# In the delta net, GpSimd's products go to ScalarE and VectorE, and a transfer that adds makes the low parts of the weights

## The chip, the cores and the metric

The kernel runs on one core of a Trainium2 chip. A time is device microseconds (us) of one launch. Five instruction streams run beside each other on the core: TensorE (PE, with its weight loads shown apart as PEld), VectorE (DVE), ScalarE (ACT), GpSimd (POOL) and SyncE (SP), which here only issues transfers. Each works through its instructions in the order in which the program lists them, and semaphores make one wait for another.

## The reference, cut to what matters

The program is two transformer blocks in float32 on 512 tokens of width 1024. The part that is changed is the second mixer of the first block, a gated delta net with 8 key heads and 16 value heads of width 128:

```python
proj = u @ w_in                                   # 1024 -> 6144 + 32
qkv = silu(causal_dwconv(proj[..., :4096], conv_w))   # four taps over the tokens
q, k = l2_norm(q) * K ** -0.5, l2_norm(k)
beta = sigmoid(b);  g = -exp(a_log) * softplus(a + dt_bias)
decay = exp(where(incl, gc[:, None] - gc[None, :], -inf))   # gc = cumsum(g)
m = where(strict, beta * (k @ k.T) * decay, 0)
u, w = triangular_solve(m + I, [v * beta, k * beta * exp(gc)])
# then the chunks in turn: v_new = u - w S;  o = q_dec S + qk v_new;  S = S g_last + k_dec^T v_new
o = rms_norm(o, norm_gain) * silu(z);   h = h + o @ w_out
```

## The kernel before, in words

Activations lie with features on the 128 partitions and the 512 tokens along the free axis. Every large product is made of three float32r matmuls of 128x512 (`mm3`): each operand is split into a high part, rounded to float32r, and a low part, what is left of it; high by high, high by low and low by high are summed in one PSUM bank. The weights come as 486 blocks of 128x1024 floats (512 KB), each holding eight 128x128 tiles. `wtile` takes a block in: SP loads it into `wr`, ACT rounds it into `wh` (the high part), DVE subtracts, `wl = wr - wh` (the low part). There are three buffers for `wr` and four each for `wh` and `wl` (`WRAW, WPART = 3, 4`), so PE can be up to three blocks behind what ACT and DVE prepare. One block feeds 24 matmuls of 128x512.

Nothing is issued while it is written: a recorder notes each operation with its operands, and a planner (`schedule`) then plays the program with a cost for each operation and fixes the order of every engine's instructions. On the chip that order holds whatever the real durations are. A changed cost or a changed instruction therefore also moves others.

The delta net (`gdn`) takes 65 of the blocks: 49 of `gdn_in` and 16 of `gdn_out`. It works in four rounds of four value heads. A round begins with `keys` for two key heads: each needs two convolutions (`conv`: DVE multiplies the projection by the norm's row R into `g`, ACT starts `y` with the tap of the current token, the three earlier taps are added, ACT takes tanh, DVE finishes the silu), transposes on PE, the decay matrices of two value heads (`G` = triangle times log-decay in a high and a low part, PE sums them in `pd`, ACT takes exp into `E`, `E` is multiplied by beta), and from E the tiles `Y`, `kqd` and `yd`. Then `inverse` solves the unit triangular systems in 31 steps on DVE (`xt`, `xp`), with `xts` and `xf` set to zero by POOL. Meanwhile PE makes the four value projections (`values`) and the output product of the round before (`project`). Last come the four heads (`gdn_head`): a recurrence over four token blocks that goes back and forth between PE, ACT (`gvn`, `ot`) and DVE (`gt`, `St`), with `kd` = keys times decay made beforehand, and the output `ot` scaled by its norm at the end, and the gates (`gates`).

Before, POOL does five kinds of product in this part: the sum of the first tap (`y + w`, with `w` made by ACT), both `G`, `E` times beta, `kd`, and the scaling of `ot`.

Of the kernel before, what the change touches and what calls it, by code (L numbers as in the profile page):

```python
# [8 lines left out]
F32 = mybir.dt.float32  # L9
F32R = mybir.dt.float32r  # L10
BF16 = mybir.dt.bfloat16
I32 = mybir.dt.int32
AF = mybir.ActivationFunctionType
ALU = mybir.AluOpType
# [3 lines left out]
S = 512  # L18
# [142 lines left out]
class Recorder:  # L161
# [104 lines left out]
    def schedule(self):  # L266
# [18 lines left out]
        while done < len(ops):  # L285
# [22 lines left out]
            T, e = best  # L308
# [48 lines left out]
                mode = op.mode  # L357
            if op.eng == "SP" or op.lat < 0:
                start = max(T + 0.1, dma_free)
                dma_free = start + op.cost  # L360
                op.end = dma_free + 2.0
                free[e] = T + 0.06
            else:
                op.end = T + cost + op.lat
                free[e] = T + cost
# [129 lines left out]
class Kernel:  # L495
    def __init__(self, tc, ctx, I, vat, cat):
        self.tc, self.nc, self.I = tc, Recorder(tc.nc), I
        self.vat, self.cat = vat, cat
        self.blocks, self.open, self.wcur = [], None, None
        self.n = 0  # L500
        self.cp = ctx.enter_context(tc.tile_pool(name="cp", bufs=1))
        self.sp = ctx.enter_context(tc.tile_pool(name="sp", bufs=2))
        self.ap = ctx.enter_context(tc.tile_pool(name="ap", bufs=NACT))
        self.pp = ctx.enter_context(tc.tile_pool(name="pp", bufs=8, space=PSUM))
        self.dp = ctx.enter_context(tc.tile_pool(name="dp", bufs=1, space=bass.MemoryType.DRAM))
# [41 lines left out]
    def wtile(self, name, k, m, width=128):  # L547
        nc = self.nc
        if not self.open or len(self.open) == 8:
            self.open = []  # L550
            self.blocks.append(self.open)
            raw = self.wide("wr", F32, ("wr", WRAW))
            hi = self.wide("wh", F32R, ("wh", WPART))
            lo = self.wide("wl", F32R, ("wl", WPART))
            n = len(self.blocks)

            for i, c in enumerate((slice(0, 256), slice(256, 1024)) if n == 1 else (slice(0, 1024),)):
                op = nc.sync.dma_start(out=raw[:, c], in_=self.I["w"][n - 1][:, c])
                if n < 3:
                    op.prio = self.loads[3 * n - 3 + 2 * i].prio + (0.5 if i or n > 1 else -0.5)  # L560
                nc.scalar.copy(hi[:, c], raw[:, c])
                nc.vector.tensor_tensor(lo[:, c], raw[:, c], hi[:, c].bitcast(F32), ALU.subtract)
            self.wcur = (hi, lo)
        j = len(self.open) * 128
        self.open.append((name, k, m))
        return self.wcur[0][:, j:j + width], self.wcur[1][:, j:j + width]
# [397 lines left out]
    def gdn(self):  # L964
# [58 lines left out]

        def conv(m):
            ps = self.gemm("gdn_in", m, xs)
            gt, y, u = self.act(name="g"), self.act(name="y"), self.act(name="w", cap=2)
            nc.vector.tensor_tensor(gt, ps, R, ALU.mult)
            w = lambda t: cw[:, t * 32 + m:t * 32 + m + 1]
            nc.scalar.activation(y, gt, AF.Identity, scale=w(3))
            nc.scalar.activation(u[:, 3:], gt[:, :S - 3], AF.Identity, scale=w(0))  # L1030
            nc.gpsimd.tensor_tensor(y[:, 3:], y[:, 3:], u[:, 3:], ALU.add)
            for t in (1, 2):
                nc.vector.scalar_tensor_tensor(y[:, t:], gt[:, :S - t], w(3 - t), y[:, t:], ALU.mult, ALU.add)
            nc.scalar.activation(gt, y, AF.Tanh)
            nc.vector.scalar_tensor_tensor(y, gt, 1.0, y, ALU.add, ALU.mult)
            return y

        def keys(j, yd):
# [33 lines left out]
            out = []  # L1072
            for i in range(2):
                h = 2 * j + i
                bc = lambda t: t[:, :, h:h + 1].broadcast_to([128, 4, 128])
                pd = self.ps((128, 4, 128))
                Gs = [self.act(F32R, name="G", shape=(4, 128), cap=4) for _ in gparts]
                for G, x in zip(Gs, gparts):
                    nc.gpsimd.tensor_tensor(G, self.c("tri").unsqueeze(1).broadcast_to([128, 4, 128]),
                                            bc(x.bitcast(F32)), ALU.mult)  # L1080
                nc.after = (len(nc.ops) - 1,)
                for part, G in enumerate(Gs):
                    nc.tensor.matmul(pd, ut, G, start=part == 0, stop=part == 1)
                nc.after = ()
                E_ = self.act(name="E", shape=(4, 128), cap=2)
                nc.scalar.activation(E_, pd, AF.Exp)
                nc.gpsimd.tensor_tensor(E_, E_, bc(beta), ALU.mult)
                Y = self.act(name="Y", shape=(4, 128))
                nc.vector.tensor_tensor(Y, E_, kk, ALU.mult)
                kqd = self.act(name="kqd", shape=(4, 128))  # L1090
# [119 lines left out]
    def gdn_head(self, h, kq, kt, vt, kqd, xf, egc, negegc, be, glb, eq):  # L1210
# [1 line left out]
        nc = self.nc  # L1212
        St = self.nc.pool_tile(self.sp, [128, 128], F32, "St", self.nm("St"), 3)
        kd = self.act(name="kd", shape=(4, 128), cap=2)
        nc.gpsimd.tensor_tensor(kd[:, 0:3], kt[:, 0:3], be[:, 0:3, h:h + 1].broadcast_to([128, 3, 128]), ALU.mult)
        ot = self.act(name="ot", shape=(4, 128), cap=3)
        ss = self.small([128, 4], "gss", bufs=3)
        for b in range(4):
# [22 lines left out]
            sq = self.nc.pool_tile(self.sp, [128, 128], F32, "gsq", self.nm("gsq"), 2)  # L1241
            nc.scalar.activation(sq, ot[:, b], AF.Square, accum_out=ss[:, b:b + 1])
        rr = self.rsqrt(ss, [128, 4], 1.0 / 128, eq)
        nc.gpsimd.tensor_tensor(ot, ot, rr.unsqueeze(2).broadcast_to([128, 4, 128]), ALU.mult)
        po = self.ps()
        for b in range(4):
            self.tr(po[:, b * 128:(b + 1) * 128], ot[:, b])
# [336 lines left out]
    def run(self, out, stages):  # L1584
# [12 lines left out]
        for s in stages:  # L1597
            if s != "swa" and ada and not hasattr(self, "cs"):
                self.ada_start()
            if s == "swa":  # L1600
                self.attention()
            elif s in ("ffn0", "ffn1"):
# [86 lines left out]
```

## Time and profile before

| | |
|---|---|
| time, median of 3 runs (lowest to highest) | 2748.89 us (2748.49 to 2749.71) |
| the profiled execution's own time | 2749.72 us |
| its span, first to last instruction | 2747.9 us |
| busy: PE, PEld, DVE, ACT, POOL | 2641.9, 2161.2, 1773.9, 1089.3, 301.7 us |
| mean granted TensorE clock | 0.983 of full |

The delta net lies at about 615 to 1210 us of the span. A granted clock of 1.00 is 2.4 GHz and 0.50 would be 1.2 GHz; a value between is a mean over both levels in that stretch. Matmuls overlap one another, so that the duration of one (385 ns) is longer than the distance between two starts. An idle time is put down to what ended it. A DVE instruction's duration is from its start to its last write, and includes the time for which it is held up by another engine at the memory.

### The profile page before, as it was taken

What the parts mean: (1) busy time and instruction counts of PE and PEld (TensorE: products, weight loads), DVE (VectorE), ACT (ScalarE), POOL (GpSimd) and SP (SyncE); (2) the same over time, 40 slices, a digit from 0 to 9 for tenths busy, and PEclk for the clock granted to TensorE, in tenths of its full rate; (3) what the DMA queues carried; (4) which work ended last, traced back from release to release, by engine and by line L of the source; (5) the groups of instructions that cost most, each with busy time, mean ns of one, the idle gap of its engine ahead of it and who ended that gap; (6) DMA issues with size and microseconds to landing.
All of it is one profiled execution on the core that took longest, in us unless ns stands there. A gap on an engine that the chain in (4) does not pass through costs nothing.

```text
span 2747.9 us, 36693 instructions
## 1 busy us (share of the span) xinstructions
PE 2641.9 (96%) x14108; PEld 2161.2 (79%) x14108; DVE 1773.9 (65%) x3576; ACT 1089.3 (40%) x1969; POOL 301.7 (11%) x333
## 2 busy tenths in 40 slices
PE   7899999997989899999999999999999999999998
PEld 5678878776768677777787898888877778988887
DVE  8977848858798889876546453334479856633334
ACT  5753323334545445543323333223264443432231
POOL 3411101104141414111001000000000000000000
PEclk9999999998899999999999999999999999999999
DMA  4115645641111121123333323233222233233231
GB/s 149 47 62 198 224 138 195 227 134 43 62 46 63 54 67 62 63 87 103 115 102 109 99 92 99 93 100 99 88 89 64 75 108 97 87 98 100 93 100 62
DMA packets 84001, 274.27 MB, mean 100 GB/s; under 512 B 9328, under 2 KB 17776, under 8 KB 83824
## 3 DMA queue, kind: packets, MB, share of 16 engines
q1 hardware_dynamic: 83680, 271.39, 30.5%
q8 instruction: 111, 1.82, 0.3%
q14 instruction: 66, 0.54, 0.1%
q10 hardware_dynamic: 144, 0.52, 0.1%
HBM read 264.54 MB, written 7.34 MB: 99 GB/s over the span
## 4 chain that ended last, share of the span: by engine, by line
PE 73%; DVE 19%; issue 3%; ACT 2%; POOL 1%; DMA 1%; SPq 0%; DVEq 0%; ACTq 0%; POOLq 0%
PE mm L406 66%; PE ps L406 8%; DVE wl L406 3%; DVE y L406 2%; DVE wa L406 1%; DVE yd L406 1%; DVE xl L406 1%; DVE g L406 1%; DVE sm L406 1%; DVE n_4t L406 1%; DVE xt L406 1%; DMA wa<-in_w_dram 1%; DVE Y L406 1%; DVE z L406 1%; POOL n_2t L406 1%
## 5 line engine op out<-in xcount | busy, mean ns | idle before, releaser
L406 PE MATMUL mm<-xh,wh 128*128 128x512 f32 (+1 forms) x3444 | 1322.7, 385 | 16.9 <-ACT xh L406 16.8
L406 PE MATMUL mm<-xl,wh 128*128 128x512 f32 (+1 forms) x3444 | 1326.2, 386 | 1.8 <-DVE xl L406 1.8
L406 PE MATMUL mm<-xh,wl 128*128 128x512 f32 (+1 forms) x3444 | 1323.8, 385 | 2.2 <-DVE wl L406 2.2
L406 PEld LDWEIGHTS mm<-xh,wh 128*128 128x128 f32 x3444 | 651.7, 189 | 142.7 <-ACT xh L406 18.6
L406 PEld LDWEIGHTS mm<-xl,wh 128*128 128x128 f32 x3444 | 652.5, 190 | 132.0 <-issue 7.5
L406 PEld LDWEIGHTS mm<-xh,wl 128*128 128x128 f32 x3444 | 652.3, 190 | 129.0 <-issue 6.3
L406 DVE TENSOR_TENSOR wl<-wr,wh 128x1024 fp32r<-128x1024 f32 (+1 forms) x415 | 521.6, 1257 | 273.9 <-issue 181.3
L406 ACT CAST wh<-wr 128x1024 fp32r<-128x1024 f32 (+1 forms) x415 | 433.6, 1046 | 414.7 <-DVE wl L406 225.3
L406 ACT CAST xh<-g 128x512 fp32r<-128x512 f32 x92 | 57.2, 622 | 250.2 <-DVE g L406 250.0
L406 DVE TENSOR_TENSOR g<-mm,g 128x512 f32<-128x512 f32 x44 | 30.4, 691 | 175.9 <-PE mm L406 175.3
L406 POOL TENSOR_TENSOR y<-y,R 128x512 f32<-128x512 f32 x48 | 67.8, 1413 | 682.8 <-ACT y L406 652.9
L406 DVE CUSTOM_DVE_ANT_0 wa<-wa,cs,vec 128x1024 f32<-128x1024 f32 x72 | 96.9, 1347 | 10.3 <-DMA wa<-in_w_dram 10.1
L406 DVE TENSOR_TENSOR xt<-xt,mm 128x512 f32<-128x512 f32 (+1 forms) x72 | 48.0, 670 | 84.2 <-PE mm L406 83.9
L406 ACT ACTIVATE sq<-xt 128x512 f32<-128x512 f32 (+1 forms) x69 | 38.7, 570 | 148.9 <-DVE xt L406 148.9
L406 DVE SCALAR_TENSOR_TENSOR xt<-mm,mod,xt 128x512 f32<-128x512 f32 (+1 forms) x47 | 31.6, 671 | 101.1 <-PE mm L406 100.8
L406 DVE TENSOR_TENSOR g<-mm,R 128x512 f32<-128x512 f32 x80 | 54.8, 685 | 56.1 <-PE mm L406 53.3
L406 DVE SCALAR_TENSOR_TENSOR y<-g,vec,y 128x511 f32<-128x511 f32 (+1 forms) x96 | 71.7, 749 | 22.8 <-ACT y L406 21.3
L406 DVE TENSOR_TENSOR g<-mm,y 128x512 f32<-128x512 f32 x48 | 33.0, 687 | 61.6 <-POOL y L406 32.2
L406 POOL TENSOR_TENSOR y<-y,w 128x509 f32<-128x509 f32 x32 | 49.5, 1547 | 209.1 <-ACT w L406 123.3
L406 DVE TENSOR_TENSOR xl<-g,xh 128x512 fp32r<-128x512 f32 x92 | 63.0, 685 | 6.9 <-ACT xh L406 6.9
L406 ACT ACTIVATE y<-g,vec 128x512 f32<-128x512 f32 x48 | 39.2, 817 | 67.4 <-DVE g L406 67.4
L406 ACT ACTIVATE g<-mm 128x512 f32<-128x512 f32 x44 | 26.4, 599 | 96.9 <-PE mm L406 96.9
(316 smaller groups left out, 2580.6 us busy)
## 6 DMA issues: line engine op xcount, KB each, us to landing
wr<-in_w_dram SPq DMA_DIRECT2D x413, 512.0 KB, 3.6
wa<-in_w_dram SPq DMA_DIRECT2D x72, 512.0 KB, 4.6
xt<-in_xt_dram SPq DMA_DIRECT2D x8, 256.0 KB, 6.3
bias<-bo SPq DMA_DIRECT2D x8, 256.0 KB, 2.7
bi<-bias SPq DMA_DIRECT2D x8, 256.0 KB, 4.4
out_dram<-fin SPq DMA_DIRECT2D x8, 256.0 KB, 2.6
bias<-bo SPq DMA_DIRECT2D x8, 192.0 KB, 1.9
bi<-bias SPq DMA_DIRECT2D x8, 192.0 KB, 3.9
```

What stands on the lines that cost most here:

```text
L406: fn(*args, **kw)
```

## The change

Six edits in the delta net, and one in the planner.

- The first tap of each convolution: the product `w` on ACT and the sum on POOL go; DVE adds this tap as it adds the other two, with a third SCALAR_TENSOR_TENSOR.
- `G`: one POOL product of 128x512 becomes four ACT products of 128x128, each with a scale per partition. There are 32 `G`.
- `E` times beta: from POOL to DVE, 16 of 128x512.
- `kd`: one POOL product of 128x384 becomes three ACT products of 128x128, for 16 heads.
- `ot` scaled: one POOL product of 128x512 becomes four ACT products of 128x128, for 16 heads.
- The low part of the 65 weight blocks of this part: DVE's subtraction goes. ACT writes `-wh` into `wl`, and POOL issues a transfer that reads the block from DRAM a second time and adds it to what lies in `wl`. 
- The planner: a transfer on POOL holds POOL for 1.1 us, counts twice its bytes and lands 3 us after.

```diff
@@ schedule
-                dma_free = start + op.cost
-                op.end = dma_free + 2.0
-                free[e] = T + 0.06
+                dma_free = start + op.cost * (2 if e == "POOL" else 1)
+                op.end = dma_free + (3.0 if e == "POOL" else 2.0)
+                free[e] = T + (1.1 if e == "POOL" else 0.06)
@@ wtile
                 nc.scalar.copy(hi[:, c], raw[:, c])
-                nc.vector.tensor_tensor(lo[:, c], raw[:, c], hi[:, c].bitcast(F32), ALU.subtract)
+                if self.by_dma:
+                    nc.scalar.activation(lo[:, c], hi[:, c].bitcast(F32), AF.Copy, scale=-1.0)
+                    nc.gpsimd.dma_start(out=lo[:, c], in_=self.I["w"][n - 1][:, c].bitcast(F32R), accum_op=ALU.add)
+                else:
+                    nc.vector.tensor_tensor(lo[:, c], raw[:, c], hi[:, c].bitcast(F32), ALU.subtract)
@@ conv
-            nc.scalar.activation(u[:, 3:], gt[:, :S - 3], AF.Identity, scale=w(0))
-            nc.gpsimd.tensor_tensor(y[:, 3:], y[:, 3:], u[:, 3:], ALU.add)
-            for t in (1, 2):
+            for t in (1, 2, 3):
                 nc.vector.scalar_tensor_tensor(y[:, t:], gt[:, :S - t], w(3 - t), y[:, t:], ALU.mult, ALU.add)
@@ keys
-                    nc.gpsimd.tensor_tensor(G, self.c("tri").unsqueeze(1).broadcast_to([128, 4, 128]),
-                                            bc(x.bitcast(F32)), ALU.mult)
+                    for b in range(4):
+                        nc.scalar.activation(G[:, b], self.c("tri"), AF.Copy, scale=x.bitcast(F32)[:, b, h:h + 1])
-                nc.gpsimd.tensor_tensor(E_, E_, bc(beta), ALU.mult)
+                nc.vector.tensor_tensor(E_, E_, beta[:, :, h:h + 1].broadcast_to([128, 4, 128]), ALU.mult)
@@ gdn_head
-        nc.gpsimd.tensor_tensor(kd[:, 0:3], kt[:, 0:3], be[:, 0:3, h:h + 1].broadcast_to([128, 3, 128]), ALU.mult)
+        for b in range(3):
+            nc.scalar.activation(kd[:, b], kt[:, b], AF.Copy, scale=be[:, b, h:h + 1])
-        nc.gpsimd.tensor_tensor(ot, ot, rr.unsqueeze(2).broadcast_to([128, 4, 128]), ALU.mult)
+        for b in range(4):
+            nc.scalar.activation(ot[:, b], ot[:, b], AF.Copy, scale=rr[:, b:b + 1])
@@ run
+            self.by_dma = s == "gdn"
```

Counted over the whole program, DVE loses 65 subtractions and gains 48 instructions, ACT loses 32 and gains 305, POOL loses 112 products and gains 65 transfers.

Three places in the order show what this does. The first is DVE in the first round, where the decay matrices of the first two heads become `Y`, `kqd` and `yd` (the numbers at the names only tell tiles apart). Before:

```order
L406 TENSOR_TENSOR Y_1145<-E_1144,kk_1137 128x512
L406 TENSOR_TENSOR kqd_1146<-E_1144,qk_1138 128x512
L406 COPY yd_1105<-Y_1145 32x128 x4
L406 TENSOR_TENSOR Y_1151<-E_1150,kk_1137 128x512
L406 TENSOR_TENSOR kqd_1152<-E_1150,qk_1138 128x512
L406 COPY yd_1105<-Y_1151 32x128 x4
L406 TENSOR_TENSOR wl_1266<-wr_1264,wh_1265 128x1024
L406 SCALAR_TENSOR_TENSOR y_1158<-g_1157,gcw,y_1158 128x511
L406 TENSOR_TENSOR g_1164<-mm_1160,R_1082 128x512
L406 SCALAR_TENSOR_TENSOR y_1158<-g_1157,gcw,y_1158 128x510
L406 TENSOR_TENSOR wl_1275<-wr_1273,wh_1274 128x1024
```

And now:

```order
L406 TENSOR_TENSOR E_1142<-E_1142,gbeta_1090 128x512
L406 TENSOR_TENSOR Y_1143<-E_1142,kk_1135 128x512
L406 TENSOR_TENSOR kqd_1144<-E_1142,qk_1136 128x512
L406 COPY yd_1105<-Y_1143 32x128 x4
L406 TENSOR_TENSOR E_1148<-E_1148,gbeta_1090 128x512
L406 SCALAR_TENSOR_TENSOR y_1156<-g_1155,gcw,y_1156 128x511
L406 TENSOR_TENSOR Y_1149<-E_1148,kk_1135 128x512
L406 TENSOR_TENSOR kqd_1150<-E_1148,qk_1136 128x512
L406 COPY yd_1105<-Y_1149 32x128 x4
L406 SCALAR_TENSOR_TENSOR y_1156<-g_1155,gcw,y_1156 128x510
L406 TENSOR_TENSOR g_1161<-mm_1157,R_1082 128x512
L406 SCALAR_TENSOR_TENSOR y_1156<-g_1155,gcw,y_1156 128x509
```

Both `wl` are gone from the list, an `E` stands ahead of each `Y`, and the convolution `y` has a third tap (128x509).

The second place is ACT, a little later in the same round, around the exponentials `E`. Before:

```order
L406 ACTIVATE E_1150<-ps_1147 128x512
L406 CAST wh_1265<-wr_1264 128x1024
L406 ACTIVATE y_1158<-g_1157,gcw 128x512
L406 ACTIVATE w_1159<-g_1157,gcw 128x509
L406 CAST wh_1274<-wr_1273 128x1024
L406 ACTIVATE E_1191<-ps_1188 128x512
```

And now:

```order
L406 ACTIVATE E_1148<-ps_1145 128x512
L406 ACTIVATE G_1185<-cst,ghi_1101 128x128 x3
L406 ACTIVATE G_1186<-cst,glo_1102 128x128 x4
L406 ACTIVATE G_1191<-cst,ghi_1101 128x128 x4
L406 ACTIVATE G_1192<-cst,glo_1102 128x128 x4
L406 ACTIVATE E_1187<-ps_1184 128x512
L406 ACTIVATE wl_1252<-wh_1251 128x1024
L406 ACTIVATE y_1162<-g_1161,gcw 128x512
```

Between two `E` there now stand fifteen small `G` products, and the negated copy `wl` of a block whose `wh` was made thirty rows earlier.

The third place is POOL, at the end of the first round's `keys`. Before:

```order
L406 TENSOR_TENSOR E_1191<-E_1191,gbeta_1090 128x512
L406 TENSOR_TENSOR E_1197<-E_1197,gbeta_1090 128x512
L406 TENSOR_TENSOR kd_1282<-kt_1120,gbe_1098 128x384
L406 TENSOR_TENSOR kd_1317<-kt_1120,gbe_1098 128x384
L406 MEMSET xp_1201 128x512
L406 COPY xp_1201<-cst 128x16 x2
L406 TENSOR_TENSOR y_1259<-y_1259,w_1260 128x509
```

And now:

```order
L406 DMA wl_1303<-in_w_dram 128x1024
L406 DMA wl_1338<-in_w_dram 128x1024
L406 MEMSET xp_1197 128x512
L406 COPY xp_1197<-cst 128x16 x2
L406 DMA wl_1373<-in_w_dram 128x1024
L406 DMA wl_1408<-in_w_dram 128x1024
L406 DMA wl_1417<-in_w_dram 128x1024
L406 DMA wl_1423<-in_w_dram 128x1024
L406 DMA wl_1462<-in_w_dram 128x1024
L406 MEMSET xts_1231 32x16x32
```

POOL's products are gone; its list in this part is the 65 transfers and the inverse's small instructions (`xp`, `xts`, `xf`) among them.

## Rows read from the trace of the kernel before

**Rows 1.** Busy us of PE, PEld, DVE, ACT, POOL; granted clock, DMA share, GB/s

```profile
600.00:1215.00 615.00, 555.85 (x3532) 457.87 (x3532) 520.21 (x1224) 296.69 (x711) 165.43 (x154) 0.94 0.19 61
```

**Rows 2.** The same view, the stretch of `keys` in each of four rounds

```profile
640.00:700.00 60.00, 47.78 (x206) 38.34 (x207) 52.77 (x102) 26.59 (x54) 25.26 (x22) 0.83 0.14 46
780.00:820.00 40.00, 28.02 (x122) 22.00 (x121) 38.58 (x70) 16.25 (x34) 19.62 (x17) 0.85 0.13 40
900.00:960.00 60.00, 49.38 (x233) 39.49 (x233) 53.16 (x100) 28.45 (x59) 26.14 (x25) 0.91 0.16 53
1040.00:1120.00 80.00, 70.18 (x348) 56.58 (x347) 74.48 (x154) 41.01 (x90) 29.88 (x23) 0.98 0.21 66
sum 240.00, PE 195.37 PEld 156.41 DVE 218.99 ACT 112.31 POOL 100.90; mean PE 48.84 PEld 39.10 DVE 54.75 ACT 28.08 POOL 25.23
```

**Rows 3.** Who waited for whom, PE and PEld, 600 to 1215: total us, times, longest

```profile
PE ps L406 <- DVE y L406: 42.0, 15, 6.0
...
PEld ps L406 <- POOL ot L406: 5.4, 6, 3.2
```

**Rows 4.** Timeline, DVE, POOL and PE, 776 to 822: start, us, what [idle before]

```profile
775.22 1.03 DVE L406 SCALAR_TENSOR_TENSOR n_4t<-n_4t,n_4e 128x4 f32<-128x4 f32 x1
...
783.48 2.21 DVE L406 COPY yd<-Y 32x128 f32<-32x128 f32 x3
...
775.18 3.12 POOL L406 TENSOR_TENSOR E<-E,gbeta 128x512 f32<-128x512 f32 x2 [0.91 <-DVE n_4t L406]
...
816.70 1.08 PE L406 MATMUL ps<-cst,y 128*128 128x128 f32 x4 [5.29 <-DVE y L406]
```

**Rows 5.** Groups of instructions, 600 to 1215: count, busy us, mean ns, idle before

```profile
L406 DVE TENSOR_TENSOR wl<-wr,wh 128x1024 fp32r<-128x1024 f32 x70 | 87.3, 1247 | 2.7 <-issue 2.2
L406 ACT CAST wh<-wr 128x1024 fp32r<-128x1024 f32 x69 | 72.1, 1046 | 66.9 <-PE mm L406 57.2 <-DVE xt L406 6.1 <-issue 2.0
L406 DVE SCALAR_TENSOR_TENSOR y<-g,gcw,y 128x511 f32<-128x511 f32 x64 | 58.4, 912 | 7.8 <-POOL y L406 7.5
...
L406 DVE COPY yd<-Y 32x128 f32<-32x128 f32 x64 | 28.4, 444 | 0.7
...
L406 ACT ACTIVATE w<-g,gcw 128x509 f32<-128x509 f32 x32 | 22.7, 710 | 0.0
...
L406 DVE TENSOR_TENSOR n_4t<-n_4y 128x4 f32<-128x4 f32 x78 | 19.4, 255 | 1.1
...
L406 DVE TENSOR_TENSOR Y<-E,kk 128x512 f32<-128x512 f32 x16 | 16.6, 1037 | 1.2 <-POOL E L406 0.9
...
L406 DVE TENSOR_TENSOR kqd<-E,qk 128x512 f32<-128x512 f32 x16 | 15.6, 977 | 0.0
```

**Rows 6.** The tiles `yd`, `y`, `n_4t` and `kqd`, 600 to 1215: duration ns min/median/max

```profile
L406 DVE COPY yd<-Y x64: 206/222/1699, 649.2 to 1096.9; 32x128 f32<-32x128 f32 x64
...
L406 DVE SCALAR_TENSOR_TENSOR y<-g,gcw,y x64: 703/747/1780, 628.5 to 1112.0; 128x511 f32<-128x511 f32 x32, 128x510 f32<-128x510 f32 x32
...
L406 DVE TENSOR_TENSOR n_4t<-n_4y x78: 149/161/1251, 615.6 to 1214.9; 128x4 f32<-128x4 f32 x78
...
L406 DVE TENSOR_TENSOR kqd<-E,qk x16: 677/685/1769, 647.8 to 1095.6; 128x512 f32<-128x512 f32 x16
```

**Rows 7.** The tile `wl` on DVE in the four stretches of rows 2

```profile
sum 240.00, DVE 33.42; mean DVE 8.36
```

**Rows 8.** Timeline of ACT, 640 to 700: four small products with a scale

```profile
684.24 1.14 ACT L406 ACTIVATE vt<-ps,gik 128x128 f32<-128x128 f32 x4 [7.14 <-PE ps L406]
```

**Rows 9.** Transfers: queue totals in 600 to 1215; issues of whole run, KB, us to landing

```profile
q1 hardware_dynamic: 10511, 37.03, 18.9%
...
wr<-in_w_dram SPq DMA_DIRECT2D x413, 512.0 KB, 3.6
...
xt<-in_xt_dram SPq DMA_DIRECT2D x8, 256.0 KB, 6.3
```

**Rows 10.** The chain that ended last, 590 to 1230: matmuls of weight blocks back to back

```profile
834.59 22.96 PE mm L406 x101
```

More of the change, by code (lines that the diff above doesn't have):

```diff
@@ L499, in __init__ @@
         self.blocks, self.open, self.wcur = [], None, None
+        self.by_dma = False
         self.n = 0
@@ L1025, in conv @@
             ps = self.gemm("gdn_in", m, xs)
-            gt, y, u = self.act(name="g"), self.act(name="y"), self.act(name="w", cap=2)
+            gt, y = self.act(name="g"), self.act(name="y")
             nc.vector.tensor_tensor(gt, ps, R, ALU.mult)
@@ L1074, in keys @@
                 h = 2 * j + i
-                bc = lambda t: t[:, :, h:h + 1].broadcast_to([128, 4, 128])
                 pd = self.ps((128, 4, 128))
```

## The prediction

> **What bounds the kernel now.** I read the busy time by stretch first. From 600 to 1215 us, where the delta net lies, PE is busy for 555.85 of 615 us at a granted clock of 0.94 [rows 1]: 59 us of waiting, and 6% of the clock, 37 us if PE had streamed all the while, are all that the change can give back, 96 us. Outside this stretch the work is the same before and after.
>
> Then I looked for where in the stretch the waiting lies. Four pieces, 240 us in all, hold 240 - 195.4 = 44.6 us of it, and the clock is lowest there, 0.83 to 0.98 [rows 2]. They are the `keys` of the four rounds. In them DVE is busy for 219 of 240 us (91%), ACT for 112, POOL for 101. The view of waits says whom PE waited for: `y`, which DVE finishes, 42.0 us in 15 waits, and then the scaled `ot` of POOL with 5.4 us [rows 3]. So DVE bounds these pieces, and PE, whose order is fixed, stands in front of a transpose of `y` although weight products lie ready behind it.
>
> The timeline of one such piece tells why DVE is late. While POOL multiplies two `E` for 3.12 us, a DVE instruction on four elements takes 1.03 us, and three copies into `yd` take 2.21 us; PE then waits 5.29 us for `y` [rows 4]. The medians of the same instructions are 0.161 and 0.222 us [rows 6]. DVE and POOL hold each other up at the memory. PE's granted clock also drops around such waits: 0.85 in the piece that holds the wait of 5.29 us [rows 2, 4].
>
> **The change part by part, DVE.** Removed in the four pieces: the subtractions into `wl`, 33.4 us [rows 7]. Removed too is what POOL's products cost DVE. Mean less median, times the count, is 64 x (444 - 222) = 14.2 us for `yd`, 64 x (912 - 747) = 10.6 for the taps of `y`, 78 x (255 - 161) = 7.3 for `n_4t`, and, with kqd's median of 685 for both tiles of one shape, 16 x (1037 - 685) = 5.6 for `Y` and 16 x (977 - 685) = 4.7 for `kqd`: 42.4 us [rows 5, 6]. Added: 32 third taps at 747 ns, 23.9 us, and 16 `E` at the 685 of `kqd`, 11.0 us [rows 6]. If all of this falls into the four pieces, DVE has 219.0 - 33.4 - 42.4 + 23.9 + 11.0 = 178 us of work in them. At its present share of 0.912 that takes 195 us.
>
> **PE.** It has 195.4 us of work in the pieces as it ran, and as little as 172 if the 23.2 us of lost clock (the lengths times one less the clock, rows 2) all come back. So PE does not hold the pieces above 195 either.
>
> **ACT.** About 27 negated copies fall into the pieces (33.4 us of subtractions at 1.247, rows 5, 7). A copy of this shape with a constant factor is not in the trace; between `w` at 0.71 us, an ACT product with half the elements, and twice that, I take the CAST of the same 128x1024, 1.046 us [rows 5]: 28 us. The 128x128 products with a scale per partition have the row of four `vt` in 1.14 us, 0.285 each [rows 8], though `vt` reads from PSUM: 128 for `G` are 36.5 us, 48 for `kd` 13.7 us. Less 32 `w`, 22.7 us [rows 5], ACT comes from 112 to 168 us. It does not bound 195 us alone, but it is now in the middle of the same chain (the taps, tanh, `E`, `G`), in one fixed queue, with up to fifteen `G` between two `E`. DVE's share of 0.912 was reached with an ACT that was half idle. I therefore put the pieces at 200 us, 5 above the two sums: a gain of 40 us. The bounds are 172, PE's work at full clock (68 us gained), and 240, nothing gained.
>
> **Elsewhere in the delta net.** The other 375 us hold 14.5 us of PE's waiting and about 14 of lost clock. POOL's `ot` goes (5.4 us of waiting, rows 3): four ACT products at 0.285, 1.14 us, stand in its place, shorter than a POOL product held up by DVE. Against it, ACT's queue, in which the recurrence's copies wait, has some 40 negated copies and 64 small products more. I take 5 us of gain, between 15 lost and 28 gained.
>
> **The adding transfer.** The trace shows none. Nor does it show a transfer issued by POOL. Each needs DRAM once more, and reads and writes SBUF. Its lower bound is a plain load of a block: 37.03 MB held the 16 DMA engines for 18.9% of 615 us, 1.65 us for 524,288 bytes, and landed 3.6 us after its issue [rows 9]. The upper bound is the slowest landing per byte, `xt` with 256 KB in 6.3 us, 12.6 us for 512 KB, taken as if all of it held the engines. I take 3.3 us, two plain loads, since it moves two operands and the row nearest in shape and source is `wr`. Then 65 transfers are 215 us beside 116 of the others, 54% of the stretch, and a block costs the DMA engines 1.65 + 3.3 = 4.95 us. PE's fastest pace is 24 matmuls at 22.96 / 101 = 0.227 us, 5.45 us a block [rows 10], so even eight blocks on end (`values` and `project`) are fed. The delay is hidden too: the new chain for a block is the negated copy, 1.05 us, the issue on POOL, which no row prices and which I bound by one of POOL's longest products, half of 3.12 us [rows 4], and 3.6 + 1.65 us to land, 7.9 us in all, while three blocks lie between, 16.3 us at PE's fastest pace. If that cover is gone, each block costs PE what the transfer exceeds it by.
>
> The page "Collectives: The Full Stack" of the Trainium skill (section "Part 3: Why 7x under link rate") says that the sum in a transfer costs nothing by itself but needs two source reads on one ring, and so runs at half the rate of a copy. By it the transfer would hold the engines for 3.3 us as well; no row here shows it.
>
> What the waits put behind them: a matmul with `wl` now waits for the transfer, and all of PE stands behind it. POOL's transfer waits for the negated copy; behind it in POOL's queue stand the next transfers and the small `xp`, `xts`, `xf`, for which DVE and ACT wait in the inverse. The negated copy waits until PE has left the block four before, but ACT already waits so for the CAST, 57.2 us in the stretch [rows 5], off the path. SP gets `wr` back earlier, after the CAST.
>
> **Sum.** 2749.72 - 40 - 5 = 2704.7 us. The profiled execution lies 0.8 us above the median of 2748.89, so I forecast 2704 us, with an own range of 2675 to 2730.
>
> **Rivals.**
>
> *The adding transfers set the pace* (chance 0.18). One stream of 65 transfers, each longer than what PE leaves it. Before, a block had 615 / 65 = 9.46 us on average; less 1.65 for the load, a transfer of more than 7.8 us makes the kernel slower than before, wherever PE waits. At 10 us the stretch takes 65 x 11.65 = 757 us, 2891 in all; at the upper bound of 12.6, 926 us and 3060. For it: no row of this kind; PE's order puts every block's third matmul behind it. Against: the loads of the same bytes take 1.65 us, so it would have to be almost five times as slow.
>
> The page "SBUF — State Buffer" (section "Who interferes with whom") of the Trainium skill speaks against the change: descriptor writing for GpSimd's transfers is starved while DVE copies in its two-port modes. By that rule the 64 copies `yd`, 14.2 us at their median, would come on top of the issues, an estimate of 0.2 us a transfer, and this rival would decide from 7.6 us on instead of 7.8; no run here shows it yet.
>
> *ACT takes DVE's place* (chance 0.16 for a small gain, 0.08 for none). If half of the 56 us that ACT gains in the pieces cannot run beside DVE (first tap, other taps, tanh and silu are one chain), the pieces take 195 + 28 = 223 us, a gain of 17 and no more: 2732. If the heads also lose the 15 us of the bound above, all is even: 2749. For it: ACT at 47% becomes 84%. Against: `G` needs nothing but the gates and can be made far ahead.
>
> *All waiting goes* (chance 0.06): pieces at 172 and the rest 15 lower, 2666. Against: no stretch of this part is free of waits today.
>
> *The edits miss the bound* is a part of the even case: PE's 42 us for `y` could be the chain's length, not DVE's load. But DVE has only some 20 idle us in 240.
>
> **Chances.** Forecast 0.52. Faster by over 0.2% (5.5 us, about what a measurement of this kernel can tell from no change) is 0.52 + 0.16 + 0.06 = 0.74. Within 0.2%: 0.08. Slower: 0.18. The range runs from 2666 to 2790: it leaves out most of the slow case above 41 us of loss, about 0.13, and a few in 100 below.
>
> **What would show it.** In the profile after: `yd` near 222 ns and `n_4t` near 161 on average; DVE in the delta net's stretch near 520 - 79 - 42 + 35, about 435 us; ACT near 410; PE's waits for `y` down from 42 to under 15; a granted clock of 0.97 or more. The forecast is wrong if PE waits for `wl`, if the transfers take over 5 us of the engines each, or if DVE's durations stay long with POOL's products gone.

## The result, and the profile after

The changed kernel takes 2688.15 us (median of 4 runs, 2685.29 to 2689.62) against 2748.69 us before (4 runs, 2748.23 to 2749.71): a ratio of 0.9777, 95% interval 0.9765 to 0.979. That is 60.5 us less, where 45 were forecast. The profiled execution after took 2689.62 us, its span is 2687.9.

Where the time came from can be read off two numbers of each page. PE's idle time, span less busy, went from 2747.9 - 2641.9 = 106.0 to 2687.9 - 2628.1 = 59.8 us, 46.2 us less. The clock lost, span times one less the mean granted clock, went from 0.017 x 2747.9 = 46.7 to 0.012 x 2687.9 = 32.3 us, 14.4 us less. This second number is an estimate, since the mean clock is rounded; PE's busy time, for the same 14108 matmuls, fell by 13.8 us. Together they are 60.6 us, where the two spans differ by 60.0.

The clock came back in the delta net alone: there, from 600 to 1215 us, about 0.06 x 615 = 37 us were lost before and 0.02 x 615 = 12 us are lost after. Ahead of it, where both kernels do the same work, this one execution lost more (0.98 against 0.99, before and then after):

```profile
0.00:600.00 600.00, 568.41 (x2820) 458.63 (x2821) 462.87 (x877) 260.23 (x446) 99.94 (x149) 0.99 0.46 154
...
0.00:600.00 600.00, 567.90 (x2800) 457.97 (x2801) 460.99 (x873) 258.28 (x445) 99.72 (x149) 0.98 0.46 154
```

Its first `n_4t` of the stretch starts at 619.8 us instead of 615.6 [rows 6], 4.2 us later, so in the two profiled executions the delta net itself gained some 64 us. Whether the other three executions after have the same loss is not shown.

The page after, first its head, then the queue of the adding transfers and their issue:

```profile
span 2687.9 us, 36962 instructions
...
PE 2628.1 (98%) x14108; PEld 2153.6 (80%) x14108; DVE 1671.5 (62%) x3559; ACT 1194.2 (44%) x2242; POOL 213.4 (8%) x286
...
q0 software_dynamic: 9360, 34.08, 7.5%
...
wl<-in_w_dram POOLq DMA_DIRECT2D x65, 512.0 KB, 5.5
```

The busy time by stretch, in the columns of [rows 1], for the delta net and for the four windows of [rows 2]. The rounds come earlier now, so that the windows no longer hold just `keys`:

```profile
600.00:1215.00 615.00, 602.21 (x3909) 496.97 (x3908) 459.28 (x1291) 429.78 (x1027) 85.04 (x113) 0.98 0.54 126
```

```profile
640.00:700.00 60.00, 56.97 (x282) 45.75 (x281) 54.96 (x148) 50.60 (x115) 9.67 (x13) 1.00 0.69 157
780.00:820.00 40.00, 38.74 (x231) 31.39 (x229) 36.20 (x99) 26.31 (x51) 7.45 (x11) 1.00 0.80 181
900.00:960.00 60.00, 57.14 (x445) 46.26 (x445) 48.02 (x131) 39.99 (x78) 11.63 (x18) 1.00 0.66 148
1040.00:1120.00 80.00, 77.36 (x608) 65.78 (x608) 58.24 (x176) 54.26 (x137) 11.65 (x16) 1.00 0.57 130
```

PE's idle time in 600 to 1215 fell from 59 us [rows 1] to 12.8, and its clock in these windows is 1.00 where it was 0.83 to 0.98 [rows 2]. Whom PE still waits for there (us, times, longest), to be set beside [rows 3]:

```profile
PE ps L406 <- DVE xt L406: 2.9, 3, 1.4
PE ps L406 <- ACT p L406: 2.6, 5, 1.2
PE ps L406 <- DVE xf L406: 1.7, 2, 1.5
PE ps L406 <- DVE y L406: 1.7, 1, 1.7
PE ps L406 <- DVE xp L406: 1.2, 1, 1.2
PE mm L406 <- DMA wl<-in_w_dram: 1.0, 1, 1.0
```

The 42.0 us for `y` are 1.7, POOL's `ot` is gone, and no other wait has taken their place. The groups of DVE and ACT that answer to [rows 5], in 600 to 1215:

```profile
L406 DVE SCALAR_TENSOR_TENSOR y<-g,gcw,y 128x511 f32<-128x511 f32 (+2 forms) x96 | 71.3, 746 | 3.3 <-ACT y L406 2.3
L406 DVE COPY yd<-Y 32x128 f32<-32x128 f32 x64 | 15.0, 235 | 0.6
L406 DVE TENSOR_TENSOR n_4t<-n_4y 128x4 f32<-128x4 f32 x78 | 12.4, 160 | 1.5
L406 DVE TENSOR_TENSOR Y<-E,kk 128x512 f32<-128x512 f32 x16 | 11.0, 688 | 0.1
L406 DVE TENSOR_TENSOR kqd<-E,qk 128x512 f32<-128x512 f32 x16 | 11.0, 686 | 0.0
L406 DVE TENSOR_TENSOR E<-E,gbeta 128x512 f32<-128x512 f32 x16 | 10.6, 688 | 0.0
```

```profile
L406 ACT CAST wh<-wr 128x1024 fp32r<-128x1024 f32 x80 | 83.5, 1045 | 36.9 <-PE mm L406 31.2 <-DVE xt L406 4.4 <-issue 1.2
L406 ACT ACTIVATE wl<-wh 128x1024 fp32r<-128x1024 f32 x65 | 68.6, 1057 | 2.3 <-PE mm L406 1.4 <-PE ps L406 0.4
L406 ACT ACTIVATE G<-cst,glo 128x128 fp32r<-128x128 f32 x64 | 21.6, 394 | 0.0
```

The means on DVE are now the medians of before within 3 ns, with kqd's 685 taken for `Y` and `E` too, and 235 against 222 for `yd` apart [rows 6]. In the tile view (duration min/median/max) the longest `n_4t` is 165 ns, where it was 1251:

```profile
L406 DVE TENSOR_TENSOR n_4t<-n_4y x78: 152/161/165, 619.8 to 1152.9; 128x4 f32<-128x4 f32 x78
```

### The profile page after: what moved, and what is told of

The parts are those of the page before. It is cut to its first block, busy times and chain, and to the rows that moved or that the text cites. A ratio compares the mean times of both kernels' runs of the same rounds, so it can differ in the third digit from the quotient of the medians.

```text
span 2687.9 us, 36962 instructions
## 1 busy us (share of the span) xinstructions
PE 2628.1 (98%) x14108; PEld 2153.6 (80%) x14108; DVE 1671.5 (62%) x3559; ACT 1194.2 (44%) x2242; POOL 213.4 (8%) x286
## 4 chain that ended last, share of the span: by engine, by line
PE 58%; DVE 2%; ACT 1%; issue 0%; POOL 0%; DVEq 0%
PE mm L406 53%; PE ps L406 5%; DVE wl L406 0%; DVE u L406 0%; DVE xl L406 0%; DVE fin L406 0%; PE mx L406 0%; ACT kmla L406 0%; DVE g L406 0%; DVE sq L406 0%; DVE y L406 0%; DVE top L406 0%; DVE kmla L406 0%; DVE xf L406 0%; DVE xt L406 0%
## 5 line engine op out<-in xcount | busy, mean ns | idle before, releaser
L406 DVE TENSOR_TENSOR wl<-wr,wh 128x1024 fp32r<-128x1024 f32 (+1 forms) x350 | 440.5, 1259 | 272.8 <-issue 173.6
L406 ACT CAST wh<-wr 128x1024 fp32r<-128x1024 f32 (+1 forms) x415 | 433.4, 1046 | 385.8 <-DVE wl L406 223.7
L406 POOL DMA_DIRECT2D wl<-in_w_dram x65 | 56.4, 867 | 455.7 <-ACT wl L406 301.0
L406 DVE SCALAR_TENSOR_TENSOR y<-g,vec,y 128x511 f32<-128x511 f32 x96 | 71.9, 749 | 23.8 <-ACT y L406 22.2
L406 DVE SCALAR_TENSOR_TENSOR y<-g,gcw,y 128x511 f32<-128x511 f32 (+2 forms) x96 | 71.3, 746 | 3.3 <-ACT y L406 2.3
L406 DVE TENSOR_TENSOR g<-mm,y 128x512 f32<-128x512 f32 x48 | 33.0, 687 | 60.5 <-PE mm L406 34.2
L406 ACT ACTIVATE wl<-wh 128x1024 fp32r<-128x1024 f32 x65 | 68.6, 1057 | 2.3 <-PE mm L406 1.4
```

What stands on the lines that cost most here:

```text
L406: fn(*args, **kw)
```

## The experiments

Two explanations fit the result. **Load:** DVE had too much to do in `keys`, and the low parts (33 us there) and the hold-ups (42 us) were taken from it; this is the prediction. **POOL's products:** what made DVE late was only that POOL multiplied beside it or ahead of it. This has two forms: the products *hold up* DVE's instructions at the memory, or the *way* of `y` and `E` through POOL's queue is long. All runs, in us; each ratio is to the kernel before as it ran beside that run (medians of 2748.32 to 2750.37); idle is span less busy of PE, "y" PE's waits for it in 600 to 1215 us, "yd" the mean of that copy there in ns:

| kernel | median | ratio, 95% interval | idle | y | yd |
|---|---|---|---|---|---|
| before | 2748.69 | 1 | 106.0 | 42.0 | 444 |
| after | 2688.15 | 0.9777 [0.9765, 0.979] | 59.8 | 1.7 | 235 |
| low_parts_only | 2751.59 | 1.0009 [0.9999, 1.0018] | 108.5 | 42.7 | 411 |
| products_moved_only | 2686.11 | 0.9771 [0.9754, 0.9787] | 64.6 | 4.1 | 248 |
| products_but_kd | 2701.45 | 0.983 [0.9813, 0.9846] | 67.6 | 3.4 | 268 |
| tap_on_pool | 2690.89 | 0.9788 [0.9774, 0.9803] | 67.4 | 12.7 | 250 |
| E_on_pool | 2684.23 | 0.9761 [0.9747, 0.9776] | 60.4 | 4.8 | 257 |
| G_on_pool | 2708.55 | 0.9852 [0.9838, 0.9867] | 85.7 | 24.0 | 353 |
| G_alone | 2736.40 | 0.9955 [0.994, 0.997] | 93.2 | 19.3 | 346 |
| pool_beside | 2707.53 | 0.9851 [0.9837, 0.9866] | 77.9 | 11.7 | 256 |
| pool_beside_same_order | 2699.14 | 0.9816 [0.98, 0.9833] | 70.0 | 7.7 | 309 |
| transfer_twice | 2719.29 | 0.9891 [0.9876, 0.9906] | 71.9 | 9.1 | 251 |
| old_transfer_cost | 2670.28 | 0.9718 [0.9703, 0.9732] | 57.1 | none | 236 |
| E_on_pool_old_cost | 2682.55 | 0.9763 [0.9748, 0.9777] | 62.4 | 2.2 | 258 |

### The low parts alone

The kernel before, with the transfers and the planner's edit, and all products left on POOL:

```diff
+                    nc.scalar.activation(lo[:, c], hi[:, c].bitcast(F32), AF.Copy, scale=-1.0)
+                    nc.gpsimd.dma_start(out=lo[:, c], in_=self.I["w"][n - 1][:, c].bitcast(F32R), accum_op=ALU.add)
```

> Only the low parts of the 65 blocks are made by the negated copy and the adding transfer; POOL keeps its five kinds of product. Load theory (DVE's work bounds the four pieces, and both its subtractions and its hold-ups count): DVE's work in them goes from 219 to 186 us, at a share of 0.912 that is 204 us, 36 us less, so about 2713 us; yd stays near 444 ns on average and n_4t near 255, since POOL still multiplies. Chain theory (the way of y and E through POOL was what PE waited for): that way is as long as before, PE still waits 40 us for y, and the time stays within 8 us of 2749. If POOL's queue delays the transfers behind its products, PE waits for wl, and it is slower than 2749.

No gain at all. The stretch, with DVE's busy time in it, then PE's waits for `y`, then the taps and `Y`:

```profile
600.00:1215.00 615.00, 554.90 (x3525) 454.58 (x3524) 457.55 (x1150) 355.47 (x776) 203.57 (x219) 0.95 0.51 116
```

```profile
PE ps L406 <- DVE y L406: 42.7, 18, 5.4
```

```profile
L406 DVE SCALAR_TENSOR_TENSOR y<-g,gcw,y 128x511 f32<-128x511 f32 x64 | 68.1, 1065 | 16.9 <-POOL y L406 16.5
...
L406 DVE TENSOR_TENSOR Y<-E,kk 128x512 f32<-128x512 f32 x16 | 20.9, 1307 | 0.6 <-POOL E L406 0.4
```

DVE lost 62.7 us of work (520.21 to 457.55), and PE waits for `y` as long as before. The taps are held up more than before (1065 ns against 912), and DVE waits 16.5 us for POOL's `y`. So, as long as POOL multiplies, DVE's load is not what PE waits for.

### The products alone

The changed kernel with DVE's subtractions back. With all five products moved and the subtractions kept, the planner finds no order that its buffers allow; so the scaling of `ot`, in the second run `kd` instead, is left on POOL. The part common to both:

```diff
-            self.by_dma = s == "gdn"
+            self.by_dma = False
```

> The products move as in the change, but for the scaling of ot, which stays on POOL; the low parts stay DVE's subtractions, and there is no adding transfer. Theory 'load' (the prediction's sum: what counts is the microseconds of DVE in the four pieces): DVE has 219 - 42 + 35 = 212 us of work left in the pieces, at 0.912 that is 232 us, a gain of 8 there and a few elsewhere: about 2735 us, PE still waiting for y for 25 to 35 us. Theory 'way' (what PE waited for is the way of y and E through POOL, a queue with products of 1.3 to 3.1 us each, and the low parts cost nothing as long as DVE is fed): most of the gain is here, 2690 to 2705 us, PE's waits for y under 12 us. Theory 'both' (either part alone leaves the chain as late as it was, since DVE and POOL take turns as the later one): 2715 to 2745.

> As products_moved_only, with kd in place of ot left on POOL (kd: 16 products of 128x384, made ahead). Theories 'hold-up' and 'way' both: as products_moved_only, 2675 to 2695 us, since the 16 products that stay are few in either case. It also tells how much the order alone moves the time.

The first gives the whole gain without a single adding transfer. That is 4 us below the range of 'way'; 'load' and 'both' are out by 29 us or more. The stretch and one window in `keys`, then PE's wait and two groups:

```profile
600.00:1215.00 615.00, 596.50 (x3893) 491.64 (x3892) 519.57 (x1358) 350.83 (x895) 46.74 (x64) 0.98 0.22 71
640.00:700.00 60.00, 58.26 (x280) 47.53 (x279) 58.57 (x136) 38.90 (x94) 0.91 (x3) 1.00 0.26 88
```

```profile
PE ps L406 <- DVE y L406: 4.1, 6, 1.5
```

```profile
L406 DVE TENSOR_TENSOR wl<-wr,wh 128x1024 fp32r<-128x1024 f32 x79 | 97.2, 1230 | 0.7 <-PE ps L406 0.3
L406 DVE SCALAR_TENSOR_TENSOR y<-g,gcw,y 128x511 f32<-128x511 f32 (+2 forms) x96 | 71.2, 743 | 0.3
```

DVE is busy for 519.57 us of the stretch, just as before (520.21), and for 98% of the window 640 to 700, yet PE waits there for 1.7 us in all. What differs is POOL: 0.91 us busy in that window instead of 25.26 [rows 2].

The second run lies 6 us above what both theories expected and is 15 us slower than the first, at a lower mean clock (0.988 against 0.993). The two differ in one POOL product for each head and in the order that the planner made. DVE is busy for 1732.4 and 1732.3 us over the whole of them, so hold-ups do not tell them apart; of the 15 us, 12 are a longer busy time of PE (2631.2 against 2619.2 us) for the same matmuls, which is clock. I take this as the order's doing; a run in which the order alone changes comes below, and it is off by 18 us. A single part undone must be read with that in mind.

### One part undone at a time

The changed kernel, each with one product back on POOL:

```diff
@@ tap_on_pool
+            nc.scalar.activation(u[:, 3:], gt[:, :S - 3], AF.Identity, scale=w(0))
+            nc.gpsimd.tensor_tensor(y[:, 3:], y[:, 3:], u[:, 3:], ALU.add)
-            for t in (1, 2, 3):
+            for t in (1, 2):
@@ E_on_pool
-                nc.vector.tensor_tensor(E_, E_, beta[:, :, h:h + 1].broadcast_to([128, 4, 128]), ALU.mult)
+                nc.gpsimd.tensor_tensor(E_, E_, beta[:, :, h:h + 1].broadcast_to([128, 4, 128]), ALU.mult)
@@ G_on_pool
-                    for b in range(4):
-                        nc.scalar.activation(G[:, b], self.c("tri"), AF.Copy, scale=x.bitcast(F32)[:, b, h:h + 1])
+                    nc.gpsimd.tensor_tensor(G, self.c("tri").unsqueeze(1).broadcast_to([128, 4, 128]),
+                                            x.bitcast(F32)[:, :, h:h + 1].broadcast_to([128, 4, 128]), ALU.mult)
```

> The changed kernel with one part undone: the first tap of each convolution is again a product w of ACT and a sum on POOL; everything else as changed. DVE has 32 taps of 0.75 us less, 24 us. Theory 'load': DVE's own work falls by 24 us and its hold-ups rise by some 10 to 15: no slower than the changed kernel, 2680 to 2692 us. Theory 'way': the chain of every convolution goes through POOL again, PE waits for y for 10 to 25 us more: 2697 to 2715 us.

> The changed kernel with one part undone: E times beta is again a POOL product (16 of them). Theory 'load': DVE has 11 us less of its own work and 16 products' hold-ups more: 2680 to 2695 us. Theory 'way': Y, kqd and yd wait for POOL, but PE needs these later than y, and DVE can go on with taps in the meantime: 2690 to 2705 us.

> The changed kernel with one part undone: G is again 32 POOL products of 128x512; ACT loses 128 small products (36 us). G needs only the gates and is made ahead, so PE does not wait for it. Theory 'load' (with hold-ups as its larger half): 32 POOL products of 1.25 us, in the pieces, bring back about a third of the hold-ups, yd's mean up from 235 to over 290 ns: 2695 to 2710 us. Theory 'way': nothing in the chain of y or E goes through POOL, so about the changed kernel's time, 2680 to 2695 us, whatever the means of DVE's instructions are.

'Way' expected a loss from the tap and from `E`, and none from `G`, and missed all three. The tap costs 2.7 us and `E` gains 3.9, less than can be told apart; `G`, for which PE does not wait, costs 20 us. All three lie in the ranges of 'load', which here rest on the hold-ups as much as on DVE's own work; that DVE's own work does not count, the runs before have shown. For the tap, though, 'way' was right on the waits: PE's waits for `y` rose by 11.0 us, where it had 10 to 25, and DVE waited 14.4 us for POOL's sum:

```profile
L406 DVE SCALAR_TENSOR_TENSOR y<-g,gcw,y 128x511 f32<-128x511 f32 x64 | 48.7, 761 | 14.9 <-POOL y L406 14.4
```

PE's idle time rose by only 7.6 us in all, and its busy time fell by 6.6 (2628.1 to 2621.5), so that little of this reached the time. For `G`, PE's waits for `y` and DVE's copies:

```profile
PE ps L406 <- DVE y L406: 24.0, 8, 4.8
```

```profile
L406 DVE COPY yd<-Y 32x128 f32<-32x128 f32 x64 | 22.6, 353 | 0.6
```

DVE's 3559 instructions are the same in number and kind as in the changed kernel, and they are busy for 1696.5 us instead of 1671.5. So 'way' cannot be all of it, since `G` costs the most and PE does not wait for it; of 'load' the hold-ups are left. What share the way has in the whole is not shown. For `G` the other side:

```diff
@@ G_alone: the kernel before, with
+                    for b in range(4):
+                        nc.scalar.activation(G[:, b], self.c("tri"), AF.Copy, scale=x.bitcast(F32)[:, b, h:h + 1])
```

> The kernel before with one part of the change alone: the 32 G of 128x512 go from POOL to 128 small products on ACT; the first tap, E, kd and ot stay on POOL, the low parts stay DVE's subtractions. Theory 'hold-up': 40 of POOL's 128 us of products go, and they are those that stand closest to E, Y and yd: a third to a half of the hold-ups, 2715 to 2735 us. Theory 'way': G was made ahead and PE never waited for it; y and E still go through POOL: 2740 to 2755 us.

12 us faster: 1.4 us above the range of 'hold-up' and 3.6 below that of 'way', so that the time alone does not decide. PE's waits for `y` fall from 42.0 to 19.3 us, which 'way' did not expect.

### Products on POOL that nobody needs

To separate the hold-ups from everything else, POOL makes products that no other engine waits for. First planned like all others, then hung onto ACT's `G` behind the planner's back, so that PE, DVE, ACT and SP keep the changed kernel's order to the last instruction:

```diff
@@ pool_beside
+                    gd = self.act(F32R, name="gd", shape=(4, 128), cap=1)
+                    nc.gpsimd.tensor_tensor(gd, self.c("tri").unsqueeze(1).broadcast_to([128, 4, 128]),
+                                            x.bitcast(F32)[:, :, h:h + 1].broadcast_to([128, 4, 128]), ALU.mult)
@@ pool_beside_same_order
+                        nc.ops[-1].calls.append((nc.nc.gpsimd.tensor_tensor, (
+                            self.spare, self.c("tri"), x.bitcast(F32)[:, b, h:h + 1].broadcast_to([128, 128]), ALU.mult), {}))
```

> The changed kernel with 32 products more on POOL: beside each G that ACT makes, POOL makes the same product into a tile that nobody reads. Nothing waits for these products except POOL's own queue. Theory 'hold-up' (POOL's products stretch DVE's instructions at the memory, and that is what G on POOL cost): yd's mean up from 235 to over 300 ns, PE's waits for y up by 10 us or more, 2700 to 2715 us. Theory 'way' (what counts is what must pass through POOL's queue before PE can go on): no instruction of the chain passes through them, 2680 to 2695 us, and if it is slower then by PE's waits for wl, since the adding transfers stand in the same queue.

> The changed kernel with the order of every instruction on PE, DVE, ACT and SP kept as it is, and 128 POOL products of 128x128 put beside the 128 small G of ACT; POOL writes them into a tile that nobody reads. The planner does not know of them. Theory 'hold-up' (POOL's products stretch DVE's instructions, and that costs time by itself): some 50 us of POOL work more, the taps, yd and n_4t longer on average, 2696 to 2712 us, PE's waits for y up by 5 us or more. Theory 'order' (the 20 us that G on POOL and the products beside it cost came from the order that the planner made of them): 2685 to 2693 us. If it is slower with waits of PE for wl, POOL's queue delayed the adding transfers, and it tells neither.

The first costs 19 us, as 'hold-up' said in time and in the waits for `y`, but not in the place: `yd` hardly changed (256 ns), the taps did (825). The second is the clean one. It costs 11 us, and its interval, 0.98 to 0.9833, lies wholly above that of the changed kernel. Its tiles, PE's waits and POOL's additional work:

```profile
L406 DVE SCALAR_TENSOR_TENSOR y<-g,gcw,y x96: 706/746/990, 625.6 to 1060.1; 128x511 f32<-128x511 f32 x32, 128x510 f32<-128x510 f32 x32, 128x509 f32<-128x509 f32 x32
```

```profile
L406 DVE TENSOR_TENSOR n_4t<-n_4y x78: 151/161/362, 615.7 to 1163.0; 128x4 f32<-128x4 f32 x78
```

```profile
PE ps L406 <- DVE y L406: 7.7, 6, 2.8
PE ps L406 <- DVE xt L406: 5.0, 2, 3.9
PE ps L406 <- DVE xp L406: 2.9, 1, 2.9
...
PE mm L406 <- DMA wl<-in_w_dram: 0.8, 1, 0.8
```

```profile
L406 POOL TENSOR_TENSOR spare<-cst,ghi 128x128 f32<-128x128 f32 x64 | 36.1, 563 | 6.2 <-DVE ghi L406 1.9
L406 POOL TENSOR_TENSOR spare<-cst,glo 128x128 f32<-128x128 f32 x64 | 35.0, 546 | 4.5
```

The medians are the old ones and the longest are longer (`n_4t` 362 ns against 165). DVE's 3559 instructions come in the same order as in the changed kernel and are busy for 1686.4 us instead of 1671.5. Set side by side one by one, the 176 that ran beside one of these products took 16.0 us more, and the other 3383 took 3.2 us less. PE's idle time rose by 10.2 us; its waits for DVE in the stretch rose from 8.6 to 18.7 us, while its matmuls wait for POOL in neither run and its wait for `wl` does not grow, so that POOL's longer queue is not the cause. Shown, then: POOL's products beside DVE cost time though nothing waits for them, here 11 us for 71 us of POOL work.

### The transfer's price and cover

```diff
@@ transfer_twice: the changed kernel, with a second adding transfer of a block of zeros for each wl
+                    nc.gpsimd.dma_start(out=lo[:, c], in_=self.I["w"][NBLK - 1][:, c].bitcast(F32R), accum_op=ALU.add)
@@ old_transfer_cost: the changed kernel, with the planner's price of a transfer on POOL as before
-                dma_free = start + op.cost * (2 if e == "POOL" else 1)
-                op.end = dma_free + (3.0 if e == "POOL" else 2.0)
-                free[e] = T + (1.1 if e == "POOL" else 0.06)
+                dma_free = start + op.cost
+                op.end = dma_free + 2.0
+                free[e] = T + 0.06
```

> As the changed kernel, with a second adding transfer behind the first for each of the 65 blocks, which adds a block of zeros: per block 3.1 us more of the DMA engines, 0.87 us more on POOL, and a chain that is longer by one landing of 5.5 us, some 14 us in all, where three blocks at PE's fastest pace are 16.3 us. If the transfers are well hidden: the time stays within 15 us of 2688; PE waits for wl under 15 us. If they are at the edge already: the engines need 1.65 + 6.2 = 7.85 us a block where PE's fastest pace is 5.45, each run of eight blocks on end loses 8 x 2.4 - 16 = 3 us and more, and with POOL's small instructions behind two transfers the inverse is late too: 30 to 100 us slower than 2688.

> As the changed kernel, but the planner counts a transfer on POOL as one on SP: once its bytes, 2 us to land, 0.06 us on POOL. Only the order of instructions changes. If the planner's new numbers matter, since the row after shows 0.87 us on POOL and 5.5 us to landing, PE now waits for wl at some blocks, 2695 to 2720 us. If the lead of three blocks hides any such error, it stays within 5 us of 2688.

Twice the transfers cost 31 us, at the lower end of 'edge', though PE waits for `wl` no longer than 'well hidden' had it. Its window 640 to 700, PE's three longest waits in the stretch, and the queue with the issue:

```profile
640.00:700.00 60.00, 53.30 (x340) 41.91 (x340) 53.18 (x141) 50.40 (x111) 16.21 (x21) 0.93 0.92 201
```

```profile
PE ps L406 <- DVE y L406: 9.1, 8, 3.3
PE ps L406 <- DVE xtd L406: 9.1, 4, 2.6
PE mm L406 <- DMA wl<-in_w_dram: 3.7, 7, 0.8
```

```profile
q0 software_dynamic: 18720, 68.17, 13.8%
...
wl<-in_w_dram POOLq DMA_DIRECT2D x130, 512.0 KB, 7.7
```

The DMA engines are full there (0.92), and a block costs them 1.65 us [rows 9] + 2 x 0.138 x 2713.1 / 130 = 7.4 us, more than PE's 5.45 [rows 10]. So one transfer is hidden and the second is not. How the second costs its 31 us is not separated: PE waits for `wl` for 3.7 us alone, and its other waits, for `y` and for `xtd` of the inverse, are longer; POOL's queue stands for 145.1 us until a first transfer has landed and the second may go; and PE's busy time is 13.1 us longer (2641.2 against 2628.1).

For the planner's price the expectation was wrong: with the old one, which is farther from what a transfer takes, the kernel is 18 us *faster* than the changed one. Span less busy differs by only 2.7 us; the clock lost is 0.007 x 2673.3 = 18.7 us instead of 32.3. Not all of that is the order's: the first tap starts at 625.0 us here and at 629.7 after, and up to there both kernels have the same order. In the profiled executions, whose spans differ by 14.6 us, some 10 are left for the order. Two windows where the small matmuls of the inverse run, after and then with the old price:

```profile
700.00:720.00 20.00, 19.25 (x250) 16.04 (x250) 7.88 (x18) 9.46 (x16) 4.04 (x8) 0.66 0.24 58
...
820.00:840.00 20.00, 18.68 (x218) 16.41 (x217) 8.35 (x20) 9.78 (x28) 3.38 (x6) 0.74 0.09 28
```

```profile
700.00:720.00 20.00, 18.81 (x213) 15.27 (x209) 8.34 (x17) 10.65 (x25) 3.83 (x8) 0.74 0.25 54
...
820.00:840.00 20.00, 20.00 (x128) 18.34 (x127) 9.45 (x44) 14.29 (x52) 1.73 (x2) 0.88 0.28 65
```

After, PE is busy nearly throughout, at a mean granted clock of 0.66 and 0.74, with 250 and 218 matmuls in 20 us, most of them small. With the old price there are fewer in each window, and less clock is lost; as the order has moved, the two windows do not hold the same pieces of work. That this is the order and not the price itself is argued from the order being all that the price can change.

To see whether the best two add:

> The changed kernel with E times beta back on POOL and with the planner's old price of a transfer on POOL; both were no slower than the changed kernel by themselves. If each gain was one of the order (where the small matmuls of the inverse come to stand among the weight products), the two need not add: 2665 to 2690 us. If they add: about 2666 us.

It has both edits, `E` on POOL and the old price. They do not add: 2682.55, slower than the old price alone. With old_transfer_cost, 2670.28, a version that beats both kernels has run.

## Why the prediction was right, and where it was not

**The direction and the waits: right.** It took 45 of PE's 59 us of waiting away and left 14; 12.8 are left. Waits for `y` under 15 us: 1.7. Clock 0.97 or more in the stretch: 0.98. That the waits came so close to the 45 us summed is in part luck: the sum reached it by counting subtractions that were worth nothing, as shown below.

**The size: the clock term was put too low.** The sum took PE's work in the pieces "as it ran", 195.4 us, and gave the clock back only in the bound of 172. The waits gave 46.2 us, the 45 of the forecast; the 14.4 us of clock are what is missing between 2704 and 2688. In the delta net it was even more, about 37 - 12 = 25 us. The low clock around the waits went with the waits; what is left of it in the delta net lies in the inverse.

**DVE bounds the pieces: wrong as a sum of load.** The step "at its present share of 0.912 that takes 195 us" treated 33.4 us of subtractions, 42.4 of hold-ups and 35 of added work as one currency. By that step the products alone would have left 219 - 42.4 + 34.9 = 211.5 us, 232 at 0.912, and a gain of some 13. They gave 63. The subtractions were worth nothing in either direction (low_parts_only, products_moved_only). With POOL's products gone, DVE was busy for 98% of a window in which PE waited for 1.7 us of 60. The argument against the rival that the edits miss the bound, "DVE has only some 20 idle us in 240", was therefore none: a busy engine can be late for another reason than its load. How much of the 60 us came through hold-ups and how much through the way of `y` and `E` in POOL's queue is not shown, nor why subtractions cost nothing. I read it so: the order was fixed with durations that know nothing of hold-ups, so these fall on the chain that PE waits for, while a subtraction has been placed where it fits, up to three blocks ahead.

**Durations.** Third taps (747 ns, measured 746), `E` on DVE (685, measured 688) and the negated copy (1046, measured 1057) were right, and so was the end of the hold-ups: the means of `n_4t`, `Y` and `kqd` are within 3 ns of the medians. Too low was ACT's `G`, taken from `vt` at 0.285 us: 21.6 / 64 = 0.34 us of busy time each. In 600 to 1215 ACT is busy for 430 us where 410 were expected, and DVE for 459 where 435 were; the stretch now also holds the first of what follows the delta net. PE waits 2.6 us for ACT's `p`. ACT did not take DVE's place.

**The adding transfer.** It holds the 16 engines for 0.075 x 2687.9 / 65 = 3.10 us (3.3 taken) and lands after 5.5 us (5.25 taken). The chain is 1.06 + 0.87 + 5.5 = 7.4 us (7.9 taken), hidden by three blocks; PE waits 1.0 us for `wl`. So the rival of the pace was rightly refused, with room for one transfer but not for two. The page "Collectives: The Full Stack" of the Trainium skill (section "Part 3: Why 7x under link rate") puts a summing transfer at half a copy's rate; here it is 3.10 / 1.65 = 1.9 plain loads, and the trace agrees. Of the starving of such transfers by DVE's copies, which the page "SBUF — State Buffer" (section "Who interferes with whom") of the Trainium skill warns of, the issues after show no sign: the 65 of them took 856 to 1034 ns, with a median of 862, and PE waited 1.0 us for `wl` in all.

**Open.** How the 60 us divide over the five products. Undoing them one by one gives -4 to +20 us, `G` alone gives 12 of 60, and the order's 10 to 18 us lie over each. A run of the low parts with DVE's hold-ups gone but POOL's chain kept was not made.

## What to carry to other kernels

An engine at 91% is not yet the bound: before relieving it of work, compare means with medians of its instructions, and ask who stretches them; here moving POOL's products away was worth all of the gain, and 65 subtractions fewer were worth none. When a wait goes, count the clock that it cost as well, from the granted clock beside it. And where a planner fixes the order, undo parts in an unchanged order, or take differences under some 18 us for no more than the order.

## What the runs showed of the hardware that was not expected

- A hold-up of `n_4t` lasts until POOL's product is done. The longest `n_4t` before, 1251 ns [rows 6], starts 0.06 us after a sum on POOL and ends 0.02 us after it:

```profile
1049.42 1.25 DVE L406 TENSOR_TENSOR n_4t<-n_4y 128x4 f32<-128x4 f32 x1
...
1049.36 1.29 POOL L406 TENSOR_TENSOR y<-y,w 128x509 f32<-128x509 f32 x1 [5.42 <-ACT w L406]
```

  All eight `n_4t` of that stretch over 300 ns end 18 to 21 ns after a product of POOL. So the size goes with the product: beside products of 1.2 us on average (pool_beside) an `n_4t` took up to 970 ns, beside those of 0.55 us (pool_beside_same_order) up to 362, with a median of 161 in both.
- The granted clock is also low where PE hardly waits: a mean of 0.66, between its levels of 1.2 and 2.4 GHz, in a stretch of 20 us in which PE was busy for 19.25, with 250 matmuls.
